# Scores of the long levels of a chunkwise gated recurrence: where they lie in PSUM, who copies them out, and how late the planner places their matmuls

## The chip, the cores and the metric

The kernel runs on one core of one Trainium2 chip, alone. The metric is the device time of one execution in microseconds (us), as a median of several runs. "PE" is TensorE (the matmul engine), "DVE" VectorE, "ACT" ScalarE, "POOL" GpSimd, "SP" SyncE, which here only issues DMAs.

## What is computed

A trunk of two layers over 256 tokens of width 1024, all in float32: layer 0 mixes tokens with a gated linear recurrence (HGRN2), layer 1 with block-sparse attention, and each is followed by a SwiGLU feed-forward. The change touches the recurrence alone. Cut to what matters, with 8 heads of 128:

```python
def hgrn2_mixer(h, w_in, w_out, lb, out_norm):
    q, fz, inp, og = split(h @ w_in)
    q = silu(q)
    f = lb + (1 - lb) * sigmoid(fz)
    k = 1 - f
    # per head: S_t = diag(f_t) S_{t-1} + (1 - f_t) i_t^T ;  o_t = S_t^T q_t
    # in chunks: scores[t, s] = sum_n q[t,n] k[s,n] prod(f[s+1..t, n]), s <= t ; o = scores @ inp + ...
    o = rms_norm(o, out_norm) * sigmoid(og)
    return o @ w_out
```

## The kernel before

**Tiling.** Every weight matrix is streamed from HBM in pieces of 128 x 1024 and split by ACT into a rounded part (`whi`, line 471) and by DVE into the remainder (`wlo`, line 473). Each product is three passes on PE: hi x hi, lo x hi, hi x lo (`mm_w`, line 580; all matmuls go through line 556). For a head h the recurrence stage first computes three projections of 24 matmuls each, by `feature_major` (line 801): forget, query and gate (loop at lines 1122 to 1127). These are "main" matmuls; they write the four PSUM banks of group B in turn. After the last head the output projection `hgrn_w_out` starts (line 1148), which takes all four banks of group B.

**The recurrence of a head.** It is not evaluated token by token but by levels m = 1, 2, 4, ..., 64, and one last product over 128 tokens. At level m, tokens in the second half of a block of 2m look at tokens of the first half. `Core.step` (line 957) builds for each level a scaled copy of the queries (`Q`) and the keys (`K`), with a few short DVE multiplications (lines 982, 996) and ACT copies (lines 984, 998), each needing the one before. Level 64 ends with three ACT instructions (lines 1006 to 1008).

**Scores.** `Core.scores` (line 1011) then issues the score matmuls of the head, `products` (line 1038): products of 32 columns of keys with the queries of one level, each of which lands in 32 partitions of a PSUM bank (`part`, line 1020). There are three score banks: `b0` holds levels 1 and 2, `b` holds levels 4, 8 and 16, `b3` holds levels 32, 64 and the 128-token product. The keys of both halves of the sequence are packed into one 128-column operand (`joint`, line 1118), so a bank holds the scores in a packed order. The wanted result is `pm`, a tile of 128 x 3 x 128 in SBUF (two of them, used in turn by even and odd heads, zeroed once on POOL at line 864). It is filled from the banks in two ways. DVE makes four predicated copies with a mask (`take`, line 1018, levels 2, 4, 8 and 16) and one of twice the size (`s0e`, line 1069, the copy is line 1071). ACT makes seven plain copies (`far`, line 1079: six blocks of 32 x 32 and 64 x 64 at line 1082, then one of 128 x 128 at line 1083). All of them write the one tile `pm`, so that the framework lets a copy of one engine wait for the copies of the other that stand before it in the program.

**Values.** The result of head h - 1 (`values`, line 1089: three matmuls of `pm` with the inputs into the bank `b4`) is issued inside `products` of head h (lines 1052 and 1053), right behind the score matmuls; for the last head it is issued by `finish` (line 1095). `result` (line 1100) then takes `b4`: DVE multiplies it with the gate (`u`, line 1106), ACT squares it for the norm (`sq`, line 707, the same PSUM bank), rounds `u` (`xh`, line 1109), DVE takes the remainder (`xl`, line 1110). `xh` and `xl` of head h are the operand of row h of `hgrn_w_out`; heads 6 and 7 are used last.

**What sets the order.** The program order of every engine is written by a planner in the kernel's own Python, class `Order` (line 158). It keeps a modelled clock of each engine; main matmuls advance `now`. Every other piece of work is an `op` with an engine, a modelled cost, its dependencies and a due time. An op is emitted when its dependencies have ended in the model. For an op of PE (`"T"`) there is a margin: it is emitted only when it has been ready for `early` ns, 1500 by default (lines 167 and 257). Engines run their instructions strictly in the order emitted. The modelled cost of DVE work is `cv(n) = (n + 66) / 0.96` ns (line 316), 202 for a `take` and 335 for `s0e`; of ACT work `ca(n) = n / 1.2 + 93` (line 320), and `far` is put at 1500 (line 1084). Score matmuls have a modelled cost of 1450 (line 1065).

```python
    def pick(self, eng, limit):
...
            t = self.ready(o)
            if t is not None and t <= limit - (o.early if eng == "T" else 0.0):
                best = (o, t)
```

Of the kernel before, what the change touches and what calls it, by code (L numbers as in the profile page):

```python
# [153 lines left out]
class Op:  # L154
    __slots__ = ("eng", "cost", "fn", "deps", "alloc", "due", "seq", "end", "nbytes", "early", "after")


class Order:
# [18 lines left out]
    def op(self, eng, cost, fn, reads=(), writes=(), alloc=(), due=0.0, nbytes=0, early=None):  # L177
        o = Op()
        o.early = self.EARLY if early is None else early
        o.after = None  # L180
        o.eng, o.cost, o.fn, o.alloc, o.nbytes = eng, cost, fn, tuple(alloc), nbytes
        o.due, o.end, o.seq = self.tile + due, None, self.seq
        self.seq += 1
        deps = []
        for b in reads:
            deps += b.writers
        for b in writes:
            deps += b.readers
        o.deps = [d for d in dict.fromkeys(deps)]
        for b in reads:  # L190
            b.readers.append(o)
        for b in tuple(writes) + o.alloc:
            b.writers.append(o)
        self.wait[eng].append(o)
        return o
# [35 lines left out]
    def emit(self, o, t):  # L231
# [6 lines left out]
        if o.nbytes:  # L238
            self.dma = max(self.dma, end) + o.nbytes / 330.0
            end = self.dma + 1900.0  # L240
        o.end = end
        self.wait[o.eng].remove(o)
# [77 lines left out]
def ca(n, ptr=0):  # L320
    return n / 1.2 + 93 + 93 * ptr
# [14 lines left out]
def hybrid_trunk(ctx: ExitStack, tc: tile.TileContext, wts, xT, par, gfin, tab, onehot, masks, out):  # L336
# [531 lines left out]
    def normed(h, b, due):  # L868
# [5 lines left out]
        return t, lambda: t.tile  # L874

    scored = {}

# [15 lines left out]
    class Core:  # L893
# [63 lines left out]
        def step(self, m, due):  # L957
            Q, K, tot = self.Q, self.K, self.tot[m]
            if m < 64:
# [35 lines left out]
                else:  # L995
                    od.op("V", cv(P), lambda: V.tensor_tensor(first(kk, m), first(kk, m), bc(1), op=OP.mult),
                          reads=[kk, tot], writes=[kk], due=due)
                od.op("A", ca(P), lambda: A.activation(  # L998
                    joint(kn, 2 * m).rearrange("p (b z i) -> p b z i", z=2, i=2 * m),
# [11 lines left out]
        def scores(self, due):  # L1011
            h, Q, K, mov = self.h, self.Q, self.K, self.mov
            pm = pms[h % 2]
            moff = {m: 2 * P + P * i for i, m in enumerate(LEVELS)}

# [8 lines left out]
            def level(b, c, m):  # L1024
                keys = joint(K[m], m)
                for g in range(4):
                    z, j, p = g % 2, g // 2, b[32 * g:32 * g + 32, :]
                    if m == 32:
                        at, to = m + 96 * z + 64 * j, c + 64 * z + 32 * j
                        part(p[:, to:to + m], keys, Q[m][:, at:at + m], g, m)  # L1030
                    else:
                        part(cut(p, c + 16 * g, (64, 2), (m, 16 // m), (1, m)), keys,
                             cut(Q[m], m + 32 * g, (P - m, 2), (2 * m, 16 // m), (1, m)), g, 32)
# [4 lines left out]
            def products():  # L1038
# [4 lines left out]
                for g in range(4):  # L1043
                    part(cut(b0[32 * g:32 * g + 32, :], 16 * g, (320, 2), (1, 16)), ones128,
                         cut(ev, EVEN.start + 16 * g, (64, 2), (1, 16)), g, 32)
                for i, m in enumerate((4, 8, 16)):
                    level(b, P * i, m)
                level(b3, 0, 32)
                for z in range(2):
                    part(b3[64 * z:64 * z + 64, P + 64 * z:P + 64 * z + 64], keys, Q[64][:, 64 + 64 * z:P + 64 * z], z, 64)  # L1050
                mm(b3[:, 2 * P:3 * P], self.kk[:, :P], self.q128.tile, start=True, stop=True)
                if before:
                    before.values()

            reads = [ev, mov, self.kk, self.q128, *K.values(), *Q.values()]
            kw = dict(reads=reads, alloc=[b0, b, b3]) if h else dict(reads=reads, writes=[b0, b], alloc=[b3])
            if before:
# [3 lines left out]
            if h == 0:  # L1061
                for t in (b0, b):
                    od.op("A", ca(384), lambda t=t: A.activation(t[:, :3 * P], pm.tile.rearrange("p a t -> p (a t)"), AF.Copy),
                          reads=[pm], alloc=[t], due=due - 25)
            o = od.op("T", 1450, products, due=due, **kw)
            if h == 0:
                o.deps += b0.writers[:1] + b.writers[:1]

            def s0e():
                v = b0[:, :384].rearrange("p (a y x) -> p a y x", a=2, y=3)[:, :, 0:3:2]  # L1070
                V.copy_predicated(pm[:, 0:3:2].rearrange("p a (x z) -> p a z x", z=2),  # L1071
                                  mk[:, :2 * P].rearrange("p (a z x) -> p a z x", a=2, z=2), v)
            od.op("V", cv(P), lambda: take(2, cut(b0, 64, (192, 2), (2, 32), (1, 2))), reads=[b0, mk], writes=[pm], due=due)
            for i, m in enumerate((4, 8, 16)):
                od.op("V", cv(P), lambda m=m, i=i: take(m, cut(b, P * i, (64, 2), (m, 64 // m), (1, m))), reads=[b, mk],
                      writes=[pm], due=due)
            od.op("V", cv(S), s0e, reads=[b0, mk], writes=[pm], due=due)

            def far():
                for r, n, a, t, c in ((0, 32, 0, 32, 0), (64, 32, 0, 96, 32), (32, 32, 2, 0, 64), (96, 32, 2, 64, 96),  # L1080
                                      (0, 64, 0, 64, P), (64, 64, 2, 0, 192)):
                    A.activation(pm[r:r + n, a, t:t + n], b3[r:r + n, c:c + n], AF.Copy)  # L1082
                A.activation(pm[:, 1, :], b3[:, 2 * P:3 * P], AF.Copy)
            od.op("A", 1500, far, reads=[b3], writes=[pm], due=due)
            self.pm = pm
# [629 lines left out]
```

## Time and profile before

| | |
|---|---|
| median of 3 runs | 620.09 us (619.45 to 620.99) |
| the profiled execution | 621.3 us, of which its span 619.5 us |
| ACT busy over the span | 415.2 us (67%) |
| POOL busy over the span | 64.9 us (10%) |
| DMA | 120.90 MB, mean 195 GB/s |
| first and last score matmul | start 52.7 us and 133.8 us |
| granted PE clock over the span | 0.992 of full speed |

The span is the time between the first and the last recorded instruction. Busy times add the recorded durations of an engine; PE matmuls overlap in a pipeline, so a busy PE is not PE at its peak. "Idle before" a row is the time for which its engine sat idle just before it, with the instruction that ended the wait; an engine that is not on the path to the end may idle at no cost. A row of a timeline gives the start, the length, the engine, the line and the operation, out <- in; with a count, several alike in a row.

### The profile page before, as it was taken

The page shows a single profiled execution, that of the slowest core. Times are in us where ns is not written, and L with a number is a line of the kernel's source. Part 1 is how long each engine was busy: PE and PEld are TensorE (multiplying, and loading weights), DVE is VectorE, ACT ScalarE, POOL GpSimd, SP SyncE. Part 2 cuts the span into 40 slices and gives each one's busy share as a digit, 9 for nine tenths or more (in the row PEclk, how much of TensorE's full clock was granted, in tenths as well). Part 3 has the DMA queues.
Part 4 walks back from the last instruction along what each step waited for, and adds up shares of the span by engine and source line. Part 5 has one row for each costly group of instructions (what it writes and reads, how often), then busy time and mean ns, then how long its engine had stood idle before and what let it go on. Part 6 is the DMA issues. An engine that isn't in the chain of part 4 may idle for free.

```text
span 619.5 us, 12693 instructions
## 1 busy us (share of the span) xinstructions
PE 596.5 (96%) x4860; PEld 563.4 (91%) x4860; DVE 517.4 (84%) x938; ACT 415.2 (67%) x818; POOL 64.9 (10%) x109
## 2 busy tenths in 40 slices
PE   8999988796999999999999999999999999999995
PEld 7899987696999999999988899999999999999984
DVE  6899878876989779889989778885879799888995
ACT  6798868864676556666756567564768566666663
POOL 0045211100201011111000100000000000000003
PEclk9999999898999999999999999999999999999998
DMA  8957432464465999889672865446566677777711
GB/s 294 338 165 238 137 105 69 157 217 138 137 204 168 193 273 250 247 236 253 206 272 89 285 204 170 138 144 207 198 203 205 184 230 238 237 235 237 205 35 68
DMA packets 35560, 120.90 MB, mean 195 GB/s; under 512 B 4811, under 2 KB 6347, under 8 KB 35500
## 3 DMA queue, kind: packets, MB, share of 16 engines
q1 hardware_dynamic: 31484, 109.05, 52.2%
q0 software_dynamic: 3056, 10.29, 10.3%
q10 hardware_dynamic: 960, 0.76, 0.4%
q8 instruction: 38, 0.62, 0.4%
q14 instruction: 22, 0.18, 0.1%
HBM read 118.71 MB, written 1.38 MB: 194 GB/s over the span
## 4 chain that ended last, share of the span: by engine, by line
PE 74%; DVE 6%; ACT 5%; issue 1%; DVEq 0%; ACTq 0%
PE psA L556 42%; PE psB L556 31%; DVE wlo L473 2%; ACT whi L471 2%; DVE bt L1018 1%; ACT bt L1082 1%; DVE ii L1362 1%; DVE bt L1071 1%; PE psB L1521 0%; ACT q L984 0%; ACT k L998 0%; PE psA L1569 0%; PE psB L1425 0%; DVE q L982 0%; DVE u L1106 0%
## 5 line engine op out<-in xcount | busy, mean ns | idle before, releaser
L473 DVE TENSOR_TENSOR wlo<-raw,whi 128x1024 fp32r<-128x1024 f32 (+1 forms) x186 | 219.5, 1197 | 30.7 <-ACT whi L471 30.5
L471 ACT ACTIVATE whi<-raw 128x1024 fp32r<-128x1024 f32 (+1 forms) x185 | 188.2, 1037 | 46.6 <-PE psA L556 21.9
L556 PE MATMUL psB<-xh,whi 128*128 128x256 f32 x608 | 169.2, 282 | 7.3 <-ACT bt L955 4.0
L556 PE MATMUL psB<-xh,wlo 128*128 128x256 f32 x608 | 167.8, 279 | 0.0
L556 PE MATMUL psB<-xl,whi 128*128 128x256 f32 x608 | 163.5, 280 | 0.0
L556 PE MATMUL psA<-xh,whi 128*128 128x256 f32 x544 | 152.0, 283 | 1.7 <-ACT xh L678 1.7
L556 PE MATMUL psA<-xh,wlo 128*128 128x256 f32 x544 | 149.4, 278 | 0.0
L556 PE MATMUL psA<-xl,whi 128*128 128x256 f32 x544 | 144.4, 278 | 0.0
L556 PEld LDWEIGHTS psB<-xh,whi 128*128 128x128 f32 x608 | 115.4, 190 | 8.5 <-ACT bt L955 4.2
L556 PEld LDWEIGHTS psB<-xh,wlo 128*128 128x128 f32 x608 | 115.4, 190 | 0.7
L556 PEld LDWEIGHTS psB<-xl,whi 128*128 128x128 f32 x608 | 112.8, 190 | 0.2 <-DVE xl L1110 0.2
L556 PEld LDWEIGHTS psA<-xh,whi 128*128 128x128 f32 x544 | 102.2, 188 | 2.8 <-ACT xh L678 1.9
L556 PEld LDWEIGHTS psA<-xh,wlo 128*128 128x128 f32 x544 | 102.3, 188 | 0.7
L556 PEld LDWEIGHTS psA<-xl,whi 128*128 128x128 f32 x544 | 99.8, 189 | 0.0
L1289 ACT ACTIVATE sgq<-sgq 128x256 f32<-128x256 f32 x44 | 18.2, 415 | 25.1 <-DVE sgq L1287 25.1
L556 PE MATMUL psB<-wlo,hh 128*128 128x512 f32 (+1 forms) x91 | 35.0, 385 | 0.0
L556 PE MATMUL psB<-whi,hh 128*128 128x512 f32 (+1 forms) x91 | 34.8, 382 | 0.1
L556 PE MATMUL psB<-whi,hl 128*128 128x512 f32 (+1 forms) x91 | 34.9, 383 | 0.0
L512 POOL DMA_DIRECT2D raw<-in_w_dram x13 | 11.7, 899 | 192.6 <-DVE wsum L504 177.4
L556 PE MATMUL psA<-whi,hh 128*128 128x512 f32 (+1 forms) x75 | 28.5, 380 | 0.3 <-DVE ii L1362 0.3
L556 PE MATMUL psA<-wlo,hh 128*128 128x512 f32 (+1 forms) x75 | 28.6, 382 | 0.0
L556 PE MATMUL psA<-whi,hl 128*128 128x512 f32 (+1 forms) x75 | 28.6, 382 | 0.0
(245 smaller groups left out, 963.4 us busy)
## 6 DMA issues: line engine op xcount, KB each, us to landing
raw<-in_w_dram SPq DMA_DIRECT2D x178, 512.0 KB, 4.3
bt<-in_w_dram SPq DMA_DIRECT2D x15, 512.0 KB, 4.5
raw<-in_w_dram POOLq DMA_DIRECT2D x13, 512.0 KB, 6.4
ii<-in_w_dram SPq DMA_DIRECT2D x9, 512.0 KB, 4.7
hT<-in_x_dram SPq DMA_DIRECT2D x8, 128.0 KB, 5.0
raw<-in_w_dram SPq DMA_DIRECT2D x4, 256.0 KB, 5.0
bt<-scr POOLq DMA_DIRECT2D x16, 64.0 KB, 7.1
bt<-in_w_dram POOLq DMA_DIRECT2D x2, 512.0 KB, 5.4
```

What stands on the lines that cost most here:

```text
L471: oa = od.op("A", ca(n), lambda h=h, r=src, o=o, n=n: A.activation(h[:, :n], r[:, o:o + n], AF.Copy), reads=[src], alloc=[h], due=due)
L473: ov = od.op("V", cv(n), lambda h=h, lo=lo, r=src, o=o, n=n: V.tensor_tensor(lo[:, :n], r[:, o:o + n], h[:, :n].bitcast(FT), op=OP.subtrac ...
L512: od.op("G", 1000, lambda: nc.gpsimd.dma_start(b.tile, wts[c0 // CHUNK], accum_op=OP.add), writes=[b], nbytes=2 * 524288, due=due + 1)
L556: T.matmul(o, a, b, start=start, stop=stop, skip_group_check=True)
L1018: V.copy_predicated(cut(pm, m, (S - m, 2), *d), cut(mk, moff[m], (64, 2), (m, 64 // m), (1, m)), src)
L1071: V.copy_predicated(pm[:, 0:3:2].rearrange("p a (x z) -> p a z x", z=2), mk[:, :2 * P].rearrange("p (a z x) -> p a z x", a=2, z=2), v)
L1082: A.activation(pm[r:r + n, a, t:t + n], b3[r:r + n, c:c + n], AF.Copy)
L1289: od.op("A", ca(S), lambda: A.activation(s.tile, s.tile, AF.Silu), reads=[s], writes=[s], due=due)
L1362: V.scalar_tensor_tensor(at(), m[:, :], c[:, tt:tt + 1], at(), op0=OP.mult, op1=OP.add)
```

## The change

Five things change, all in the recurrence.

1. Level 16 moves from bank `b` to bank `b3`. Its keys are no longer packed: the copy of line 998 for m = 8 writes them at their own places into a tile of 128 x 256 whose other columns are zero. Two such tiles are made once, zeroed once on POOL (`zeroed`) and used in turn (`alternate`). Level 16 then takes 8 score matmuls in place of 4 (both halves of the keys for each of four groups), 16 columns wide each.
2. In `b3` the scores of levels 16, 32, 64 and the 128-token product now lie as they lie in `pm`, 3 x 128 columns. The rest of `b3` is zeroed by an ACT copy for head 0, as `b0` and `b` were before.
3. `far` is one ACT copy of 128 x 384 from `b3` over the whole of `pm`.
4. DVE's masked copies (levels 2, 4 and 8, and `s0e`; that of level 16 is gone) come after this copy, by an explicit dependency, and their modelled cost is 170 ns higher each.
5. In the planner, the score matmuls get `early=2800` in place of 1500, a modelled cost of 1600 in place of 1450, and a new `lag` of 1200: what depends on them is planned as if they ended 1200 ns later.

```diff
@@ -152,7 +152,7 @@
 
 
 class Op:
-    __slots__ = ("eng", "cost", "fn", "deps", "alloc", "due", "seq", "end", "nbytes", "early", "after")
+    __slots__ = ("eng", "cost", "fn", "deps", "alloc", "due", "seq", "end", "nbytes", "early", "after", "lag")
 
 
 class Order:
@@ -177,7 +177,7 @@
     def op(self, eng, cost, fn, reads=(), writes=(), alloc=(), due=0.0, nbytes=0, early=None):
         o = Op()
         o.early = self.EARLY if early is None else early
-        o.after = None
+        o.after, o.lag = None, 0.0
         o.eng, o.cost, o.fn, o.alloc, o.nbytes = eng, cost, fn, tuple(alloc), nbytes
         o.due, o.end, o.seq = self.tile + due, None, self.seq
         self.seq += 1
@@ -238,7 +238,7 @@
         if o.nbytes:
             self.dma = max(self.dma, end) + o.nbytes / 330.0
             end = self.dma + 1900.0
-        o.end = end
+        o.end = end + o.lag
         self.wait[o.eng].remove(o)
         for b in o.alloc:
             if isinstance(b.ring, Slots):
@@ -873,6 +873,13 @@
               alloc=[t], due=due)
         return t, lambda: t.tile
 
+    turn = [rings["k16"].make() for _ in range(2)]
+
+    def alternate():
+        turn.append(turn.pop(0))
+        return turn[1]
+    rings["k16"].make = alternate
+    zeroed = od.op("G", 1400, lambda: [G.memset(t, 0.0) for t in turn], due=0)
     scored = {}
 
     def score_bank(h, i):
@@ -995,6 +1002,11 @@
                 else:
                     od.op("V", cv(P), lambda: V.tensor_tensor(first(kk, m), first(kk, m), bc(1), op=OP.mult),
                           reads=[kk, tot], writes=[kk], due=due)
+                if m == 8:
+                    at = lambda t: cut(t, 0, (4 * m, 32 // m), (P + 2 * m, 2), (1, 2 * m))
+                    od.op("A", ca(P), lambda: A.activation(at(kn), at(kk), AF.Copy), reads=[kk], alloc=[kn],
+                          due=due + .2).deps.append(zeroed)
+                    return
                 od.op("A", ca(P), lambda: A.activation(
                     joint(kn, 2 * m).rearrange("p (b z i) -> p b z i", z=2, i=2 * m),
                     cut(kk, 0, (4 * m, 32 // m), (P + 2 * m, 2), (1, 2 * m)), AF.Copy), reads=[kk], alloc=[kn], due=due + .2)
@@ -1011,7 +1023,7 @@
         def scores(self, due):
             h, Q, K, mov = self.h, self.Q, self.K, self.mov
             pm = pms[h % 2]
-            moff = {m: 2 * P + P * i for i, m in enumerate(LEVELS)}
+            moff = {2: 2 * P, 4: 3 * P, 8: 4 * P}
 
             def take(m, src):
                 d = ((2 * m, 64 // m), (1, m))
@@ -1026,8 +1038,12 @@
                 for g in range(4):
                     z, j, p = g % 2, g // 2, b[32 * g:32 * g + 32, :]
                     if m == 32:
-                        at, to = m + 96 * z + 64 * j, c + 64 * z + 32 * j
+                        at, to = m + 96 * z + 64 * j, 2 * P * z + 64 * j + m * (1 - z)
                         part(p[:, to:to + m], keys, Q[m][:, at:at + m], g, m)
+                    elif m == 16:
+                        for z in range(2):
+                            at, to = m + 32 * g + (P - m) * z, 2 * P * z + 32 * g + m * (1 - z)
+                            part(p[:, to:to + m], K[m][:, P * z:P * z + P], Q[m][:, at:at + m], g, 32)
                     else:
                         part(cut(p, c + 16 * g, (64, 2), (m, 16 // m), (1, m)), keys,
                              cut(Q[m], m + 32 * g, (P - m, 2), (2 * m, 16 // m), (1, m)), g, 32)
@@ -1043,45 +1059,44 @@
                 for g in range(4):
                     part(cut(b0[32 * g:32 * g + 32, :], 16 * g, (320, 2), (1, 16)), ones128,
                          cut(ev, EVEN.start + 16 * g, (64, 2), (1, 16)), g, 32)
-                for i, m in enumerate((4, 8, 16)):
+                for i, m in enumerate((4, 8)):
                     level(b, P * i, m)
-                level(b3, 0, 32)
+                for m in (16, 32):
+                    level(b3, 0, m)
                 for z in range(2):
-                    part(b3[64 * z:64 * z + 64, P + 64 * z:P + 64 * z + 64], keys, Q[64][:, 64 + 64 * z:P + 64 * z], z, 64)
-                mm(b3[:, 2 * P:3 * P], self.kk[:, :P], self.q128.tile, start=True, stop=True)
+                    to = 2 * P * z + 64 * (1 - z)
+                    part(b3[64 * z:64 * z + 64, to:to + 64], keys, Q[64][:, 64 + 64 * z:P + 64 * z], z, 64)
+                mm(b3[:, P:2 * P], self.kk[:, :P], self.q128.tile, start=True, stop=True)
                 if before:
                     before.values()
 
             reads = [ev, mov, self.kk, self.q128, *K.values(), *Q.values()]
-            kw = dict(reads=reads, alloc=[b0, b, b3]) if h else dict(reads=reads, writes=[b0, b], alloc=[b3])
+            kw = dict(reads=reads, alloc=[b0, b, b3]) if h else dict(reads=reads, writes=[b0, b, b3])
             if before:
                 before.b4 = score_bank(h - 1, 3)
                 kw["reads"] += [ii, before.pm]
                 kw["alloc"].append(before.b4)
             if h == 0:
-                for t in (b0, b):
+                for t in (b0, b, b3):
                     od.op("A", ca(384), lambda t=t: A.activation(t[:, :3 * P], pm.tile.rearrange("p a t -> p (a t)"), AF.Copy),
                           reads=[pm], alloc=[t], due=due - 25)
-            o = od.op("T", 1450, products, due=due, **kw)
+            o = od.op("T", 1600, products, due=due, early=2800.0, **kw)
+            o.lag = 1200.0
             if h == 0:
-                o.deps += b0.writers[:1] + b.writers[:1]
+                o.deps += b0.writers[:1] + b.writers[:1] + b3.writers[:1]
+
+            od.op("A", ca(3 * P), lambda: A.activation(pm.tile.rearrange("p a t -> p (a t)"), b3[:, :3 * P], AF.Copy),
+                  reads=[b3], writes=[pm], due=due)
+            far = pm.writers[-1]
 
             def s0e():
                 v = b0[:, :384].rearrange("p (a y x) -> p a y x", a=2, y=3)[:, :, 0:3:2]
                 V.copy_predicated(pm[:, 0:3:2].rearrange("p a (x z) -> p a z x", z=2),
                                   mk[:, :2 * P].rearrange("p (a z x) -> p a z x", a=2, z=2), v)
-            od.op("V", cv(P), lambda: take(2, cut(b0, 64, (192, 2), (2, 32), (1, 2))), reads=[b0, mk], writes=[pm], due=due)
-            for i, m in enumerate((4, 8, 16)):
-                od.op("V", cv(P), lambda m=m, i=i: take(m, cut(b, P * i, (64, 2), (m, 64 // m), (1, m))), reads=[b, mk],
-                      writes=[pm], due=due)
-            od.op("V", cv(S), s0e, reads=[b0, mk], writes=[pm], due=due)
-
-            def far():
-                for r, n, a, t, c in ((0, 32, 0, 32, 0), (64, 32, 0, 96, 32), (32, 32, 2, 0, 64), (96, 32, 2, 64, 96),
-                                      (0, 64, 0, 64, P), (64, 64, 2, 0, 192)):
-                    A.activation(pm[r:r + n, a, t:t + n], b3[r:r + n, c:c + n], AF.Copy)
-                A.activation(pm[:, 1, :], b3[:, 2 * P:3 * P], AF.Copy)
-            od.op("A", 1500, far, reads=[b3], writes=[pm], due=due)
+            for n, fn in ((P, lambda: take(2, cut(b0, 64, (192, 2), (2, 32), (1, 2)))),
+                          (P, lambda: take(4, cut(b, 0, (64, 2), (4, 16), (1, 4)))),
+                          (P, lambda: take(8, cut(b, P, (64, 2), (8, 8), (1, 8)))), (S, s0e)):
+                od.op("V", cv(n) + 170, fn, reads=[b0, b, mk], writes=[pm], due=due).deps.append(far)
             self.pm = pm
             if before:
                 before.result()
```

## The prediction

> **What bounds the kernel now.** I read the page first, for the span and the share of PE.
>
> ```profile
> span 619.5 us, 12693 instructions
> PE 596.5 (96%) x4860; PEld 563.4 (91%) x4860; DVE 517.4 (84%) x938; ACT 415.2 (67%) x818; POOL 64.9 (10%) x109
> ```
>
> PE is busy for 596.5 of 619.5 us, so what can be won lies in the places where PE idles. Next I cut the span into stretches. Columns: stretch, its length, then busy time and (instructions) of PE, PEld, DVE, ACT and POOL, then the granted PE clock, the DMA share and GB/s.
>
> ```profile
> 52.00:83.00 31.00, 29.71 (x458) 28.52 (x456) 24.93 (x63) 24.49 (x81) 9.45 (x21) 1.00 0.48 161
> 83.00:144.00 61.00, 49.59 (x596) 47.16 (x596) 47.61 (x111) 44.82 (x143) 8.28 (x22) 0.97 0.42 134
> 118.00:122.00 4.00, 4.00 (x74) 3.67 (x75) 3.46 (x10) 3.62 (x10) 0.46 (x1) 0.59 0.46 135
> 144.00:149.00 5.00, 4.88 (x26) 4.72 (x27) 2.06 (x4) 0.06 (x1) 0.69 (x1) 0.66 0.78 275
> ```
>
> In the first half of the recurrence (52 to 83) PE is busy for 29.7 of 31 us. In the second half (83 to 144) it is busy for 49.6 of 61: 11.4 us are lost. Neither DVE (47.6) nor ACT (44.8) is full either, so no single engine is the bound there. The two short stretches come after PE's long waits; in them the granted clock is 0.59 and 0.66.
>
> Who made PE wait, from the view of waits (us in total, times, longest):
>
> ```profile
> PE psB L556 <- ACT bt L955: 4.0, 1, 4.0
> PE psB L556 <- ACT xh L1109: 3.3, 1, 3.3
> PE psA L556 <- ACT k L1008: 2.4, 4, 0.9
> PE psA L1021 <- ACT q L984: 0.7, 1, 0.7
> PE psA L1021 <- ACT bt L998: 0.7, 1, 0.7
> PE psA L556 <- ACT sq L707: 0.7, 1, 0.7
> PE psA L1021 <- DVE bt L1071: 0.6, 1, 0.6
> PE psA L1021 <- ACT k L998: 0.5, 1, 0.5
> ```
>
> These eight rows add up to 12.9 us. Nearly all are waits for ACT: for operands of the score matmuls (`k`, `q`, `bt`: lines 998, 1008, 984), for the gate's sigmoid that frees a PSUM bank (line 955, 4.0 us at one place) and for the last head's `xh` (line 1109, 3.3 us). The chain that ended last, for 83 to 144, says what made ACT late:
>
> ```profile
> by line: ACT whi L471 14.1%; DVE wlo L473 12.4%; DVE bt L1018 10.9%; issue 10.3%; ACT bt L1082 9.4%; DVE bt L1071 6.0%; ACT q L984 4.1%; ACT k L998 3.1%; DVE q L982 2.9%; DVE u L1106 2.8%; DVE k L996 2.6%; ACT xh L1109 2.2%; ACT k L992 1.7%
> ```
>
> No PE entry is among the costly ones: for 61 us the path to the end runs through ACT and DVE. The copies from the score banks into `pm` (L1018, L1082, L1071) make up 26.3% of it, 16.0 us; the splitting of weights (L471, L473) 26.5%. The queues of one head, in the timelines, show how these copies cost more than their own length. ACT first, then DVE:
>
> ```profile
> 87.65 1.24 ACT L1082 ACTIVATE bt<-psA 32x32 f32<-32x32 f32 x6
> 88.90 0.28 ACT L1083 ACTIVATE bt<-psA 128x128 f32<-128x128 f32 x1
> ...
> 91.78 0.39 ACT L707 ACTIVATE sq<-psA 128x256 f32<-128x256 f32 x1 [2.61 <-DVE u L1106]
> ```
>
> ```profile
> 89.21 1.52 DVE L1018 COPY_PREDICATED bt<-mk,psA 128x128 f32<-128x128 uint8 x4 [1.81 <-ACT bt L1083]
> 90.76 0.74 DVE L1071 COPY_PREDICATED bt<-mk,psA 128x256 f32<-128x256 uint8 x1
> 91.30 0.46 DVE L1106 SCALAR_TENSOR_TENSOR u<-psA,pv,bt 128x256 f32<-128x256 f32 x1
> ```
>
> Since all copies write `pm`, the two engines take turns. DVE stands idle for 1.81 us until ACT's seven copies (1.24 + 0.28) are done; then ACT stands idle for 2.61 us until DVE's five masked copies and `u` are done, because the squares read the bank that `u` reads. From 87.65 to 91.76 (the end of `u`) is 4.1 us in which the two engines do one engine's work. The groups of 52 to 144 (busy, mean ns | idle before) show that this holds for all heads:
>
> ```profile
> L1018 DVE COPY_PREDICATED bt<-mk,psA 128x128 f32<-128x128 uint8 x32 | 10.8, 336 | 8.7 <-ACT bt L1083 7.5
> L1082 ACT ACTIVATE bt<-psA 32x32 f32<-32x32 f32 (+1 forms) x48 | 9.5, 197 | 5.6 <-DVE bt L1018 5.2
> L1083 ACT ACTIVATE bt<-psA 128x128 f32<-128x128 f32 x8 | 2.2, 278 | 0.1
> L707 ACT ACTIVATE sq<-psA 128x256 f32<-128x256 f32 x6 | 2.3, 386 | 10.1 <-DVE u L1106 10.1
> ```
>
> **The change part by part.**
>
> *One copy in place of seven.* The trace has no copy of 128 x 384 from PSUM, but it has one of the same size into PSUM, and one of 128 x 128 from PSUM, that of L1083 above (278 ns).
>
> ```profile
> L1063 ACT ACTIVATE psA<-bt x2: 472/472/473, 37.9 to 38.4; 128x384 f32<-128x384 f32 x2
> ```
>
> With the difference of these two, 194 ns for 256 elements, a copy out of PSUM is bounded by 0.47 us and, if PSUM were dearer to read at that size than to write, by three times 0.28 = 0.84 us. I take 0.47, the row of equal size. ACT loses 1.24 + 0.28 - 0.47, about 1.05 us a head.
>
> *One masked copy less.* Four took from 89.21 to 90.76, 1.55 us, the first being dearer than the rest; three take about 1.2. The one of twice the size stays (0.74, of which 0.54 to the start of `u`), and so does `u` (0.46).
>
> *The order of the two engines.* ACT's copy is now always first, so DVE always waits for it, and never the other way. A head's section is then 0.47 + 0.05 of hand-over + 1.2 + 0.54 + 0.46 = 2.7 us against 4.1: 1.4 us less. The saving is about the same where DVE's four copies stood first before and ACT waited, as in the last head (DVE, then ACT):
>
> ```profile
> 135.19 1.52 DVE L1018 COPY_PREDICATED bt<-mk,psA 128x128 f32<-128x128 uint8 x4
> ...
> 138.62 0.45 DVE L1106 SCALAR_TENSOR_TENSOR u<-psA,pv,bt 128x256 f32<-128x256 f32 x1
> ```
>
> ```profile
> 136.80 1.25 ACT L1082 ACTIVATE bt<-psA 32x32 f32<-32x32 f32 x6 [3.00 <-DVE bt L1018]
> ```
>
> Here the section ran from 135.19 to 139.07, 3.9 us, with ACT idle for 3.00. Between 83 and 144 there are five such sections, the first and the last of which are shown: 5 x 1.4 = 7.0 us come off the path. The cross-check by the chain: L1018's 10.9% of 61 us (6.6) falls by a quarter, 1.7; L1082's 9.4% (5.7) falls to five copies of 0.47, by 3.4; together 5.1, without L1083 and the hand-overs. I take 7.0 and keep 5.1 as the lower end. In the first half, PE idles for 1.3 us only, so there the same saving buys no time; it lets DVE and ACT arrive less late at 83, which is the upper end: a sixth section, 8.4.
>
> PE's own waits of 12.9 us are this same time seen from the other side; I don't count them again.
>
> *More score matmuls.* Level 16 gets 4 matmuls more a head. Their price is read from PE's rows:
>
> ```profile
> 61.05 0.54 PE L1021 MATMUL psA<-q,k 128*32 128x32 f32 x32
> 61.51 0.34 PE L1021 MATMUL psA<-q,bt 128*64 128x64 f32 x4
> ```
>
> 32 of them took from 61.05 to 61.51, 14 ns each: 4 x 8 x 14 ns = 0.5 us in all. The Trainium skill, "TensorE: Matmul & The Clock Gate", section "Wait — 56ns, not 53.3ns?", says that start to start never falls below about 25 ns however narrow the matmul is; by that the 32 added ones would cost 0.8 us in place of 0.5, an estimate. The trace's 14 ns disagree with that floor, and the trace decides. Behind 83 PE has 11.4 us of idle time that covers them; before that it has nearly none: 3 heads x 4 x 14 ns, 0.2 us, which I add.
>
> *Zeroing and the unpacked keys.* The third zero copy of head 0 costs ACT 0.47 us once, at a time (about 38 us) when PE has main matmuls to do; it counts nothing, and 0.5 if that cover fails. POOL's two zeroed tiles:
>
> ```profile
> 24.49 0.77 POOL L864 MEMSET bt<- 128x384 f32 x2
> ...
> 37.39 0.40 POOL L929 TENSOR_TENSOR tot<-ff 128x128 f32<-128x128 f32 x1 [12.13 <-ACT ff L915]
> ```
>
> Two tiles of 384 columns took 0.77 us, so two of 256 take about 0.5, in a gap of 12.1 us before POOL's next work: nothing. The copy of the keys has the same number of elements as before.
>
> *Later in the order.* `early` is 1300 ns longer: PE gets about 1.3 us more of main work before a head's score matmuls, and does not stand for their operands. `lag` puts the copies out of the banks up to 1.2 us later in the queues of ACT and DVE, behind splits of weights that have to be done anyway. In the middle of the stage this changes what stands in front, not how much there is. The planner's cost for the five masked copies was 4 x 202 + 335 = 1143 ns against 2.1 us in the trace; now it is 3 x 372 + 505 = 1621 against 1.2 + 0.74 = 1.9. So the plan runs 0.3 us a head ahead of the chip in place of 1.0, and places operands and readers more truly. At the end of the stage, though, being later costs:
>
> ```profile
> 133.09 0.33 PE L1021 MATMUL psA<-mov,k 128*32 128x32 f32 x16
> ...
> 138.61 0.28 PE L556 MATMUL psB<-xl,whi 128*128 128x256 f32 x1
> 144.12 0.38 PE L556 MATMUL psB<-xh,whi 128*128 128x256 f32 x1 [3.30 <-ACT xh L1109]
> ```
>
> The last head's score matmuls start at 133.09; PE has main work until 138.9, and at the end waits 3.3 us for `xh` of that head, until 144.12. If those matmuls come 1.3 us later while the main work left is the same, the chain behind them starts 1.3 us later, and by a weight split more if the lag lets one in (up to 1.2). I take 1.3 and keep 0 and 2.5.
>
> *Sum.* -7.0 + 1.3 + 0.2 = -5.5 us. The profiled execution took 621.3 us (span 619.5 and 1.8 around it); it becomes 615.8. The median of the runs shown is 620.09, 1.2 below the profiled one, so the forecast is **614.6**. Its own bounds: 8.4 saved and no loss at the end, 611.9; 5.1 saved, 2.5 lost and 0.5 for PE, 618.0.
>
> **The rivals.**
>
> *PE becomes the bound.* With the copies short and PE's work placed later, all waits but half of the tail's 3.3 could close: 12.9 - 1.6 - 0.5 = 10.8 us, so 609.3. For it speaks that DVE and ACT are at three quarters in 83 to 144; against it that they hold the whole chain there and lose only 1.4 us a head.
>
> *The long gaps shrink, and with them the slow clock.* Behind the 3.3 us wait at the end, PE ran 5 us at 0.66, on the path: 1.7 us. If the gap becomes short enough that the clock is kept, the forecast falls by that, to 612.9. The stretch at 118 (0.59) lies beside the ACT and DVE chain and gives nothing. The Trainium skill, "TensorE: Matmul & The Clock Gate", section "Why this matters for your kernels", asks for no idle gaps over some 3 us between bursts, else the clock halves; both gaps here are longer and both were followed by a slow clock, so the trace agrees. Against it: the end is just the place where the change starts later.
>
> *Nothing to be measured.* The 1.4 us a head become idle time of ACT and DVE, since other waits come last: splits of weights pulled ahead by the lag, or the chain of `q` and `k` copies, which makes up the rest of the path. Then 620.1 less about 0.5: 619.6.
>
> *Slower: the end of the stage.* The gate's sigmoid and the rows of heads 6 and 7 are what the output projection waits for. If later score matmuls and later copies put `xh` of head 7 back by the whole 1.3 + 1.2 us, and the savings of the heads before are spent in waiting for the same ACT queue, the time is 620.1 + 2.5 + 0.5 = 623.1. It decides once the savings that reach 133 us are less than 3.0 us, about two sections of the five. For it: PE's cover behind the last score matmuls is only some 4 us. Against it: the same section is 1.4 us shorter there too.
>
> **How the numbers follow.** What can be told from no change is 0.3%, 1.9 us. Chances: forecast 0.50, PE the bound 0.13, kept clock 0.11, nothing 0.15, slower 0.11. So faster by over 0.3% has 0.74, within 0.15, slower 0.11. The likeliest case alone spans 611.9 to 618.0. The range for 8 in 10 goes from 608.5, a little below the PE-bound case, to 620.5, which takes in the case of nothing and leaves the slower one out.
>
> **What would show it.** Right: one ACT copy of 128 x 384 a head at about 0.47 us in place of L1082 and L1083; three rows of `take` behind it; sections from this copy to the end of `u` of about 2.7 us; ACT's idle time before `sq` down from 10.1 to some 6 us; PE busy over 54 of the 61 us or the stage ending near 138.5 in place of 144; waits for L1008, L984 and L998 nearly gone. Wrong: these are seen, but PE's waits for L955 or L1109 have grown by as much, or a wait of PE for `bt` or `b3`'s reader has taken their place; or the copy takes 0.8 us and more.

## The result, and the profile after

The changed kernel takes 613.0 us (median; 610.72 to 614.73), the kernel before 620.23 us (619.45 to 620.99) beside it. The ratio is 0.9881 (0.9846 to 0.9916): 7 us faster. The profiled execution took 610.72 us with a span of 608.9; that is 10.6 us below the profiled one of before, so the two profiles differ by somewhat more than the medians. Two versions below, fourth_copy and before_far_first_old_costs, had one slow execution each (744.04 and 661.62 us, at granted clocks of 0.751 and 0.849), which their medians and ratios leave out.

The same stretches as before, in the kernel after (stretch, its length, busy time and instructions of PE, PEld, DVE, ACT, POOL, then the granted PE clock, the DMA share and GB/s):

```profile
52.00:83.00 31.00, 31.00 (x444) 30.19 (x444) 28.54 (x68) 27.11 (x82) 14.26 (x25) 1.00 0.59 195
83.00:144.00 61.00, 54.36 (x719) 51.45 (x717) 46.88 (x107) 37.85 (x103) 7.68 (x19) 0.94 0.44 142
134.00:139.00 5.00, 4.97 (x21) 4.72 (x22) 1.23 (x4) 0.00 (x0) 0.70 (x1) 0.50 0.51 199
144.00:149.00 5.00, 4.34 (x38) 4.35 (x39) 5.00 (x11) 4.91 (x10) 0.00 (x0) 1.00 0.20 77
```

In the first half PE has no idle time left (31.00 of 31). In the second it is busy for 54.4 of 61 us, against 49.6. ACT has 7.0 us less work there (37.85 against 44.82), some of which has moved into the first half (27.11 against 24.49). The last stretch now belongs to the feed-forward: the stage's work is over before 144. Between 134 and 139 the granted clock is 0.50.

PE's waits between 40 and 160 us, in the kernel after (us in total, times, longest):

```profile
PE psB L556 <- ACT xh L1124: 2.7, 2, 1.5
PE psB L556 <- DVE mov L949: 1.8, 1, 1.8
PE psA L556 <- ACT xh L678: 1.7, 1, 1.7
PE psB L556 <- DVE xl L1125: 0.8, 1, 0.8
PE psB L556 <- ACT bt L962: 0.2, 1, 0.2
```

No operand of the score matmuls is waited for any more (lines 984, 998 and 1008 of before). The sigmoid of the gate (line 955 before, 962 now) costs 0.2 in place of 4.0 us, the last heads' `xh` 2.7 in place of 3.3. New are 1.8 us for `mov`, the DVE product that frees a PSUM bank of the query projection, and 0.8 us for the last head's `xl`.

What became of the copies, from the groups of 40 to 144 (busy, mean ns | idle before):

```profile
L1030 DVE COPY_PREDICATED bt<-mk,psA 128x128 f32<-128x128 uint8 x24 | 8.4, 349 | 1.6 <-ACT bt L1088 0.7
L1094 DVE COPY_PREDICATED bt<-mk,psA 128x256 f32<-128x256 uint8 x8 | 6.0, 744 | 0.3
L1088 ACT ACTIVATE bt<-psA 128x384 f32<-128x384 f32 x8 | 3.8, 480 | 0.5 <-PE psA L556 0.4
L707 ACT ACTIVATE sq<-psA 128x256 f32<-128x256 f32 x6 | 2.3, 382 | 4.8 <-DVE u L1121 4.6 <-PE psA L556 0.2
```

The taking of turns is over: DVE stood idle for 8.7 us ahead of its `take` copies (7.5 of it for ACT), now 1.6; ACT for 5.6 us ahead of its copies, now 0.5; ahead of `sq` 10.1, now 4.8. One head's queues show how, DVE first, then ACT:

```profile
99.20 0.48 DVE L1121 SCALAR_TENSOR_TENSOR u<-psA,pv,bt 128x256 f32<-128x256 f32 x1
99.59 0.42 DVE L949 TENSOR_TENSOR mov<-psB,sgq 128x256 f32<-128x256 f32 x1
100.06 1.12 DVE L1030 COPY_PREDICATED bt<-mk,psA 128x128 f32<-128x128 uint8 x3
101.22 0.74 DVE L1094 COPY_PREDICATED bt<-mk,psA 128x256 f32<-128x256 uint8 x1
```

```profile
99.55 0.48 ACT L1088 ACTIVATE bt<-psA 128x384 f32<-128x384 f32 x1
99.92 0.38 ACT L707 ACTIVATE sq<-psA 128x256 f32<-128x256 f32 x1
100.18 0.42 ACT L1124 ACTIVATE xh<-u 128x256 fp32r<-128x256 f32 x1
```

`u` stands ahead of the masked copies, not behind them. While ACT copies, DVE does `u` and `mov`; the squares and `xh` then follow on ACT without a wait, while DVE does its masked copies. The prediction had `u` last.

Where the time went, by the first wait of the feed-forward (`xh`, line 678), which ends at 153.83 us before and here:

```profile
144.66 0.39 PE L556 MATMUL psA<-xh,whi 128*128 128x256 f32 x1 [1.73 <-ACT xh L678]
```

From 40 us to that point PE is idle for 14.6 us before (113.83 less 99.27 busy) and for 7.3 after (104.66 less 97.37). Of the 9.2 us by which the point comes earlier, 7.3 are idle time of PE; the other 1.9, and 1.4 us outside the stage, were not followed.

### The profile page after: what moved, and what is told of

The parts are those of the page before. It is cut to its first block, busy times and chain, and to the rows that moved or that the text cites. A ratio compares the mean times of both kernels' runs of the same rounds, so it can differ in the third digit from the quotient of the medians.

```text
span 608.9 us, 12763 instructions
## 1 busy us (share of the span) xinstructions
PE 593.3 (97%) x4924; PEld 561.0 (92%) x4924; DVE 514.0 (84%) x930; ACT 407.8 (67%) x771; POOL 68.3 (11%) x111
## 4 chain that ended last, share of the span: by engine, by line
PE 81%; DVE 8%; DMA 6%; ACT 2%; issue 2%; POOL 0%; DVEq 0%; ACTq 0%; POOLq 0%
PE psB L556 46%; PE psA L556 33%; DMA raw<-in_w_dram 5%; DVE wlo L473 3%; ACT whi L471 1%; PE psA L1033 1%; DMA ii<-in_w_dram 1%; DVE wsum L504 1%; DVE ii L1377 1%; DVE hl L1326 1%; DVE wdiff L499 0%; PE psB L1536 0%; PE psA L1584 0%; PE psB L1440 0%; DVE sgq L1302 0%
```

## The experiments

Each ratio is to the kernel before, run beside it. The first two split the change: the later order without the new layout, and the new layout without the later order.

**order_only.** The kernel before, with the edit to the planner alone:

```diff
-            o = od.op("T", 1450, products, due=due, **kw)
+            o = od.op("T", 1450, products, due=due, early=2800.0, **kw)
+            o.lag = 1200.0
```

> The kernel before with the planner's change alone (early 2800, lag 1200); scores, banks and copies as before. If the shorter turn of ACT and DVE made the gain, this stays at 618 to 622 us, and ACT still waits about 10 us for u before its squares. If the later order made it, 613 to 616, and PE's waits for operands of the score matmuls (4.9 us before) are gone.

625.76 us, ratio 1.0079 (1.0050 to 1.0107): slower by 5, outside both of the ranges expected. The two largest of PE's waits in 40 to 160 us:

```profile
PE psB L556 <- DVE mov L942: 9.9, 3, 4.2
PE psA L1021 <- DVE bt L1072: 2.4, 1, 2.4
```

`mov` (line 942 in this kernel) reads the query projection's bank; three times PE stood before that bank, with main work that the longer margin had put ahead of the score matmuls, until DVE came to it (up to 72.82, 86.34 and 123.35 us). In 100 to 128 us the granted clock was 0.78. From 40 us to the first wait of the feed-forward PE is idle for 17.3 us in place of 14.6, and the granted clock is 0.91 in place of 0.97, so much of the loss is clock that went with the waits.

**layout_only.** The kernel after, without that edit:

```diff
-            o = od.op("T", 1600, products, due=due, early=2800.0, **kw)
-            o.lag = 1200.0
+            o = od.op("T", 1600, products, due=due, **kw)
```

> The kernel after with early and lag as they were before (1500 and 0); layout, one ACT copy and modelled costs as after. If the shorter turn made the gain, 613 to 615.5 us, with some waits of PE for operands of the score matmuls back. If the later order made it, 618 to 620.

605.85 us, ratio 0.9752 (0.9717 to 0.9786): 15 us faster than before, 7 faster than the whole change, and below both of the ranges expected. Its stretches:

```profile
100.00:128.00 28.00, 28.00 (x409) 27.10 (x408) 22.89 (x51) 19.19 (x51) 3.03 (x7) 1.00 0.52 164
128.00:154.00 26.00, 22.01 (x182) 21.14 (x181) 21.13 (x36) 14.77 (x26) 2.83 (x3) 1.00 0.46 155
```

The kernel after, in the same stretches:

```profile
100.00:128.00 28.00, 25.97 (x394) 24.75 (x393) 24.79 (x59) 20.09 (x57) 2.46 (x8) 1.00 0.42 128
128.00:154.00 26.00, 20.73 (x149) 19.63 (x148) 17.13 (x32) 12.43 (x23) 0.70 (x1) 0.87 0.31 108
```

PE works through 100 to 128 us without a gap, and the clock stays at 1.00 to the end of the stage. The feed-forward's first wait ends at 138.92, 5.74 us before that of the kernel after. PE's idle time from 40 us on is 4.0 in place of 7.3, 3.3 less; the slow clock of the kernel after (0.87 over 26 us) is worth 3.4 more. Together that is 6.7, one more than the 5.7 us between the two profiled executions (610.72 and 604.99). By place, 1.9 us are lost by the start of the last head's score matmuls (122.19 here, 124.07 in the kernel after) and 3.9 behind it, where the slow clock lies. Part of the gain over the kernel before is clock, too: over the whole span it was 0.983 to 0.994 in the eleven executions of before and 0.994 to 0.999 in the six of layout_only, 0.988 and 0.996 on average. By that difference, up to some 5 of the 15 us are slow clock that is gone, an estimate.

**no_lag** and **no_margin** undo one half each of that edit in the kernel after: the first leaves out the line with `lag`, the second the argument `early=2800.0`.

> The kernel after with lag 0 and early still 2800. If the lag is what took back 7 us of the layout's gain (it delays the copies and what stands behind them, such as the copy that frees the query's PSUM bank), this is near 606 us; if the wider margin took it back, near 613.

> The kernel after with early back at 1500 and lag still 1200. The counterpart: near 613 us if the lag is to blame, near 606 if the margin is. If each does half, both are near 609.

no_lag: 610.7 us, ratio 0.9831 (0.9809 to 0.9854). no_margin: 606.44 us, ratio 0.9777 (0.9747 to 0.9807). The first lies between the two values expected, the second at one of them. So the margin alone costs about 5 us over layout_only, and the lag alone nothing that shows (606.44 against 605.85, within the intervals). On top of the margin the lag comes out at some 2.3 us more, but the intervals overlap (0.9809 to 0.9854 against 0.9846 to 0.9916), so this is not shown. The waits of no_lag and their places show what the margin does:

```profile
PE psB L556 <- ACT xh L1123: 2.5, 1, 2.5
PE psB L556 <- ACT bt L962: 2.1, 1, 2.1
```

As in the kernel after (the wait for `mov`, up to 109.02), a wait falls at a change of projection, at 108.70: PE has done the main work that the margin put first and now stands before a PSUM bank whose reader is late. In the kernel after that sigmoid ran at 109.78 and `mov` at 108.46, in layout_only at 106.44 and 104.77. The main matmuls are the same number in both; taken earlier, they are missing later.

**layout_last_late** asks whether the margin hurts where the prediction put its cost, at the end of the stage. layout_only, with margin and lag for the last head alone:

```diff
-            o = od.op("T", 1600, products, due=due, **kw)
+            o = od.op("T", 1600, products, due=due, early=2800.0 if h == NH - 1 else None, **kw)
+            o.lag = 1200.0 if h == NH - 1 else 0.0
```

> The kernel after with early 1500 and lag 0, but 2800 and 1200 for the last head alone: its score matmuls come 12 main matmuls (1.4 us) later in PE's order. By the prediction's term, 1.3 us more than layout_only: 607.2. If the longer wait at the end also costs PE its clock, 3 to 5 us more: 609 to 611. If the margin hurts in the middle heads and not here, 605.9.

605.41 us, ratio 0.9757 (0.9730 to 0.9784): the same as layout_only. Being later in the last head alone costs nothing that shows, though the 1.3 us of the prediction would lie within the intervals. The 7 us come with the margin of the heads before.

**layout_values_now** goes at the last wait of layout_only, 2.25 us for `xh`: the last head's `values` without the margin of 1500 ns.

```diff
-            od.op("T", ct(S) + ct(P), self.values, reads=[ii, self.pm], alloc=[self.b4], due=0)
+            od.op("T", ct(S) + ct(P), self.values, reads=[ii, self.pm], alloc=[self.b4], due=0, early=0.0)
```

> The kernel after with early 1500 and lag 0, and the last head's values issued as soon as the planner has them ready (early 0 in place of 1500 for this one op): they move ahead of six main matmuls. In layout_only PE issued them 1.1 us after the last masked copy, and waits 2.2 us at the end of the stage. If that wait is the end's chain, 0.5 to 1.5 us less than layout_only: 604.5 to 605.5. If the splits of weights set the end, the same 605.8.

606.27 us (602.34 to 608.32), ratio 0.9763 (0.9725 to 0.9801): no difference from layout_only. The wait did shrink, to 1.73 us, but in the profiled execution the clock was lost behind it (last section).

**layout_costs_old** asks whether truer costs in the plan were part of the gain. layout_only, with the costs of before:

```diff
-            o = od.op("T", 1600, products, due=due, **kw)
+            o = od.op("T", 1450, products, due=due, **kw)
...
-                od.op("V", cv(n) + 170, fn, reads=[b0, b, mk], writes=[pm], due=due).deps.append(far)
+                od.op("V", cv(n), fn, reads=[b0, b, mk], writes=[pm], due=due).deps.append(far)
```

> The kernel after with early 1500 and lag 0, and the modelled costs of the masked copies and of the score matmuls as before (170 ns less each, 1450); the dependency on ACT's copy stays. If true costs in the plan make the order's part of the gain, PE waits for operands come back: 608 to 612. If the dependency alone makes it, 605 to 607.

603.16 us (602.63 to 606.23), ratio 0.9734 (0.9708 to 0.9760). Truer costs bring nothing; this is the fastest version measured, 16.7 us below the kernel before beside it, though its interval overlaps that of layout_only.

Now the layout's 15 us. **seven_copies** and **fourth_copy** put the two removed costs back, at the same modelled cost, into the kernel after.

```diff
-            od.op("A", ca(3 * P), lambda: A.activation(pm.tile.rearrange("p a t -> p (a t)"), b3[:, :3 * P], AF.Copy),
-                  reads=[b3], writes=[pm], due=due)
+            def seven():
+                flat = pm.tile.rearrange("p a t -> p (a t)")
+                for c, n in ((0, 32), (32, 32), (64, 32), (96, 32), (128, 64), (192, 64), (256, 128)):
+                    A.activation(flat[:, c:c + n], b3[:, c:c + n], AF.Copy)
+            od.op("A", ca(3 * P), seven, reads=[b3], writes=[pm], due=due)
```

```diff
-                          (P, lambda: take(8, cut(b, P, (64, 2), (8, 8), (1, 8)))), (S, s0e)):
+                          (P, lambda: [take(8, cut(b, P, (64, 2), (8, 8), (1, 8))) for _ in range(2)]), (S, s0e)):
```

> The kernel after with the one ACT copy cut into seven that move the same 384 columns, at the same modelled cost, so that the order of all engines is that of after; ACT pays about 1 us more a head. If the short copy made the gain, five to six heads give back 1 us each: 617 to 619 us. If the order made it and the copy has slack now, at most 1 us: 613 to 614.

> The kernel after with the masked copy of level 8 done twice in a row, at the same modelled cost; DVE pays 0.3 us more a head, the order is the same. If DVE's part of the turn is on the path, 5 x 0.3 = 1.5 us: about 614.5. If it has slack, 613.

seven_copies: 613.12 us, ratio 0.9867 (0.9835 to 0.9899). fourth_copy: 613.69 us, ratio 0.9875 (0.9844 to 0.9906). Neither differs from the kernel after. The first was weaker than meant: the seven pieces took 0.84 us a head, 0.36 more than the one copy, not the 1 us counted on. And in the kernel after, copies have slack, since PE's waits there come from the margin. So the question was put again where they have none.

**layout_copy4.** layout_only, with the ACT copy done four times in a row at the same modelled cost:

```diff
-            od.op("A", ca(3 * P), lambda: A.activation(pm.tile.rearrange("p a t -> p (a t)"), b3[:, :3 * P], AF.Copy),
+            od.op("A", ca(3 * P), lambda: [A.activation(pm.tile.rearrange("p a t -> p (a t)"), b3[:, :3 * P], AF.Copy) for _ in range(4)],
```

> The kernel after with early 1500 and lag 0, and the ACT copy done four times in a row at the modelled cost of one: the order of all engines stays, and ACT's share of a turn is about as long as the seven copies of before (0.47 + 3 x 0.4 = 1.7 us). If the short copy makes the layout's gain, it gives back 6 to 10 us: 612 to 616. If not, 606 to 608.

612.33 us, ratio 0.9870 (0.9833 to 0.9907): 6.5 us of the 15 are gone, with the main matmuls in the same order as in layout_only. The four copies took 2.04 us a head, 1.57 more than one and 0.5 more than the seven copies of before, so the length of ACT's copy does matter here, and yet the kernel stays 8.7 us ahead of before.

**before_far_first** looks for those 8.7 us. The kernel before, with its layout, its seven copies and its five masked copies; but `far` is planned first, and each masked copy depends on it, with the 170 ns more of modelled cost. **before_far_first_old_costs** is the same without the 170.

```diff
+            first_far = od.op("A", 1500, far, reads=[b3], writes=[pm], due=due)
...
-            od.op("V", cv(S), s0e, reads=[b0, mk], writes=[pm], due=due)
...
-            od.op("A", 1500, far, reads=[b3], writes=[pm], due=due)
+            od.op("V", cv(S) + 170, s0e, reads=[b0, mk], writes=[pm], due=due).deps.append(first_far)
```

> The kernel before (its layout, seven ACT copies, four masked copies, early 1500, no lag), but ACT's copies first by an explicit dependency and the masked copies planned 170 ns dearer each, as in after. If the gain comes from the length of the copies (1.4 us a head), this stays at 618 to 622 us. If it comes from the fixed and truly planned order of the two engines, most of the layout's 15 us appear: 607 to 612.

> The kernel before with ACT's seven copies first by an explicit dependency, and the modelled costs as before. The run with the dearer modelled costs took 612.4 us. If the dependency alone makes that gain, 611 to 614; if it needs the truer costs, 616 to 621.

612.44 us, ratio 0.9862 (0.9839 to 0.9886), and 612.49 us, ratio 0.9866 (0.9836 to 0.9896). One dependency in the plan is worth 7 to 8.5 us, with no copy shortened. It does two things at once: the planner now knows of the wait, and ACT's copies come first in every head, where before DVE's stood first in some (the last head, for one). The two were not taken apart. The groups of before_far_first in 40 to 150 us:

```profile
L1018 DVE COPY_PREDICATED bt<-mk,psA 128x128 f32<-128x128 uint8 x32 | 10.8, 337 | 2.0 <-ACT bt L1073 1.1
L1072 ACT ACTIVATE bt<-psA 32x32 f32<-32x32 f32 (+1 forms) x48 | 9.5, 197 | 2.7 <-PE psA L556 2.1
L1078 DVE COPY_PREDICATED bt<-mk,psA 128x256 f32<-128x256 uint8 x8 | 5.9, 743 | 0.3
L707 ACT ACTIVATE sq<-psA 128x256 f32<-128x256 f32 x6 | 2.3, 382 | 2.6 <-DVE u L1107 2.6
```

The same copies of the same length as before, but the idle time ahead of `take` is 2.0 in place of 8.7, ahead of `sq` 2.6 in place of 10.1. The plan of before did not know that copies which write one tile wait for each other: an op depends on writers of what it reads and on readers of what it writes, not on other writers. So it could set masked copies at the head of DVE's queue, where they stood until ACT was done. With the dependency it gives DVE other work first. In one head:

```profile
63.59 0.48 DVE L1107 SCALAR_TENSOR_TENSOR u<-psA,pv,bt 128x256 f32<-128x256 f32 x1
63.98 0.28 DVE L996 TENSOR_TENSOR k<-k,tot 128x128 f32<-128x128 f32 x1
64.18 0.28 DVE L982 TENSOR_TENSOR q<-q,tot 128x128 f32<-128x128 f32 x1
64.38 0.41 DVE L942 TENSOR_TENSOR mov<-psB,sgq 128x256 f32<-128x256 f32 x1
64.72 1.21 DVE L473 TENSOR_TENSOR wlo<-raw,whi 128x1024 fp32r<-128x1024 f32 x1
65.85 1.46 DVE L1018 COPY_PREDICATED bt<-mk,psA 128x128 f32<-128x128 uint8 x4
```

ACT's seven copies run from 63.93 to 65.45 meanwhile; DVE loses nothing to them.

## Why the prediction came out

Forecast 614.6 us, measured 613.0, inside the likeliest case's own bounds (611.9 to 618.0). But the sum was right through two errors of opposite sign, each about as large as the answer. The number was luck in good part.

- **One copy in place of seven.** Right: 0.478 us against 0.47 predicted, and the upper bound of 0.84 can be dropped. **One masked copy less**: three took 1.11 to 1.19 us, against 1.2.
- **The order of the two engines: -7.0.** The direction was right, the size wrong: with the later order taken out, the rest of the change is worth 15 us. The step held that a head's section still runs through both engines in a row, copy, `take`, `s0e`, `u`, only shorter: 2.7 in place of 4.1 us. In the trace there is no such section left: `u` goes beside ACT's copy, the squares beside the masked copies. About 7 to 8.5 of the 15 us come with the dependency in the plan alone (the two runs of before_far_first), with the copies as long as ever; about 6.5 more from the rest of the layout, which layout_copy4 takes away by lengthening the copy. Its 1.57 us a head is more than the 1.05 that the change saved, so copy length alone may be worth less than 6.5; the split was not made finer. Counting five sections also missed that PE's idle time in the first half (1.3 us) went as well.
- **More score matmuls: +0.2.** The count was off by a factor of two: the trace has two records for each of these matmuls (32 a head for the 16 that the program issues at levels 4 to 32, now 40 for 20), so four more matmuls are eight more records. In the last head the group's records and the step to the next group took 0.42 us before (133.30 to 133.72) and 0.53 after (124.28 to 124.80), 0.1 a head in place of 0.06, or 0.3 in three heads. That is still small, and no run took them by themselves. **Zeroing** did not show among PE's waits.
- **Later in the order: nothing in the middle, +1.3 at the end.** This is the step that failed, at both places. "In the middle of the stage this changes what stands in front, not how much there is" is true of PE's work, but the prediction drew from it that nothing is lost. Main matmuls write banks that are freed by DVE and ACT, and work done early runs into a bank that is not free yet. On top of the new layout margin and lag cost 7 us. In the two profiles 1.9 of 5.7 us are lost up to the last head's score matmuls and 3.9 behind them, where three waits of 3.5 us in all stand in place of one of 2.25 and the clock is lost for 3.4 us. The prediction's own reason for a cost at the end, that the last head comes later, does not show by itself (layout_last_late, where 1.3 us could hide in the noise). How the margin of the heads before reaches the end was not followed. Against the kernel before the tail is no longer than it was: the last head's score matmuls start at 124.07, 9.0 us earlier, and the stage ends 9.2 earlier. The truer costs, thought to help the plan, did not.

The rivals. "Nothing to be measured" is excluded by the interval. "PE becomes the bound" is what the layout by itself does in the middle of the stage (28.00 busy of 28 us), and at 605.85 it goes further than the 609.3 it was priced at; in the change as made it was undone by the margin. "The clock is kept" holds in the profile of layout_only, not in that of the kernel after. "Slower: the end of the stage" named the right edit and the wrong place: the edit does make the kernel before slower by 5 us, through waits in the heads before the last and the clock lost with them. Among the signs listed, the waits for lines 984, 998 and 1008, PE's busy time (54.4, though some 3.7 of it are the slow clock, 0.94 over 61 us) and `sq`'s idle time (4.8, for some 6) came out; a section of 2.7 us did not exist. `sq`'s wait is a sign of turn-taking, not a measure of time: in layout_copy4 it is 0.6 us, and that kernel is slower than layout_only by 6.5.

## What to carry to other kernels

Where a planner writes the order, look first for waits that the hardware queue will have and the plan doesn't know, such as two engines writing one tile: one dependency gave as much here as the rest of the new layout. A margin that makes an engine "not wait" by giving it other work first only moves the wait, if that work needs buffers which the late engines free. And split a change that has a layout and a schedule in it: here the schedule gave back half of what the layout won.

## What the runs showed of the hardware

**The clock falls after shorter gaps than expected, and not always.** In layout_values_now PE waited 1.73 us, up to 129.50, and then ran at half clock for over 6 us (stretches of 2 us):

```profile
128.00:130.00 2.00, 0.50 (x3) 0.34 (x3) 1.21 (x3) 1.45 (x3) 0.00 (x0) 1.00 0.78 213
130.00:132.00 2.00, 2.00 (x10) 2.00 (x10) 1.38 (x2) 0.00 (x0) 0.00 (x0) 0.51 0.77 311
...
136.00:138.00 2.00, 2.00 (x16) 2.00 (x15) 1.49 (x2) 0.99 (x4) 0.00 (x0) 0.79 0.00 0
```

In layout_only it waited 2.25 us at the same place, up to 130.77, and kept it:

```profile
130.00:132.00 2.00, 1.23 (x8) 1.05 (x9) 1.53 (x4) 0.42 (x1) 0.00 (x0) 1.00 0.97 383
132.00:134.00 2.00, 2.00 (x19) 2.00 (x19) 0.16 (x1) 0.00 (x0) 0.69 (x1) 1.00 0.79 303
```

So the length of the gap alone does not decide. The Trainium skill, "TensorE: Matmul & The Clock Gate", section "Why this matters for your kernels", asks that gaps stay under some 3 us; these runs lost the clock after 1.73 us, order_only kept it after 3.10 us (up to 86.34), and the measurement decides.

The traces tell the cases apart. In each of the 14, all changes of the granted clock fall on a grid of 3.41 us, whose place differs from one execution to the next (the kernel before: 117.89, 121.31, 145.20 and 148.61 us). The stretches of the grid in which the two waits lie, first in layout_values_now, then in layout_only:

```profile
126.61:130.02 3.41, 1.68 (x13) 1.30 (x11) 2.40 (x5) 1.63 (x3) 0.00 (x0) 1.00 0.46 125
```

```profile
126.64:130.05 3.41, 1.88 (x15) 1.63 (x13) 2.80 (x5) 1.39 (x2) 0.00 (x0) 1.00 0.31 59
130.05:133.46 3.41, 2.69 (x21) 2.51 (x22) 1.64 (x5) 0.42 (x1) 0.15 (x1) 1.00 0.97 375
```

The shorter wait lies in one stretch, in which PE is busy for 49%; the clock falls at its end. The longer one lies across a boundary, and PE is busy for 55% and 79%. Between 20 and 590 us the 14 traces show 18 falls from full clock. PE was busy for under 46% of the stretch before 15 of them, and for 49 to 54% before the other three; no stretch at full clock under 46% was without a fall, and several of 47 to 53% were. So where a gap lies counts with its length, and the line is near half of a stretch. No run moved a gap on purpose.

A loss of two such stretches is worth 3.4 us (0.87 over 26 us). Single executions of one version spread by more, with the clock: layout_values_now gave 602.34 us at 0.999 over the span and 608.32 at 0.993. Differences of 2 or 3 us between versions of this kernel should be read with that in mind.

**Copies in a row overlap or not.** ACT's seven copies of 32 x 32 to 128 x 128 from different partitions took 1.53 us in before; seven column pieces over all 128 partitions, with more elements in all (49152 against 28672), took 0.82 to 0.87; four copies of 128 x 384 onto the same tile 2.04, 0.51 apart, with no overlap. The number of instructions was a poor guide to the price.
